# The last two attention units of a double-buffered einsum, loaded whole instead of in two halves

## The chip, the cores and the metric

The kernel runs on one core of a Trainium2 chip. The metric is the device time of one execution in microseconds; a kernel's time is the median of its runs. The profile is one further execution, recorded by the hardware profiler; its times count from the start of its own span.

## The reference

```python
batch, n_heads, seq, head_dim = 8, 12, 1024, 64
attn_weights: (8, 12, 1024, 1024) float32
v:            (8, 12, 1024, 64)   float32
out = np.einsum('bhqs,bhsd->bhqd', attn_weights, v).astype(np.float32)
```

For each of 96 heads, a 1024 x 1024 matrix of weights is multiplied by a 1024 x 64 matrix of values. The weights are 403 MB of float32, v and the output 25 MB each. There are few operations for each byte of the weights.

## The kernel before, in words

**Tiles.** Four heads make a group q, of which there are NV = 24. A group's weights are loaded as 128 partitions (4 heads x 32 row blocks), each with 32 rows of 1024. Half of that, G = 16 row positions, is one *unit* n; there are NU = 48 units, and unit n belongs to group n // 2. A unit is 8 MB of float32 in HBM; its load converts to bf16 on the way and writes 4 MB into `abf[n % 2]` (line 100), of which there are two. An even unit has i = 0, an odd one i = 1.

**What happens to a unit** (`pe_unit`, line 199). TensorE waits for the load (`s_abf`, line 201). It transposes the 16 positions, in 64 matmuls that go by line 144; pairs of bf16 are moved as one float32 word. Ahead of position GH = 8 it waits for `s_half` (line 204). VectorE and ScalarE copy the transposed tiles from PSUM to `at` (line 277). In an even unit, TensorE then spreads the four heads' v over partitions (line 161), and the copies of line 250 put it into `vbf`. Then it transposes the products of the unit before back (line 174), which ScalarE copies into `osb` (line 258) and counts in `s_out`, one for each unit. Last come the products of this unit (line 189), copied to `ot` by line 289. After unit 47 one more back transpose follows, whose two copies count in `s_fin`.

**Loads.** All loads of weights are issued from GpSimd's queue (POOL) by `load_attn` (line 341). The load of unit n + 2 is issued when the transposes of unit n have ended (line 396), because they free its buffer. So while a unit is worked on, the next one's load is under way. Units from `HALVED` on are loaded in two transfers of 8 row positions: the first counts in `s_abf`, the second in a semaphore of its own, `s_second[n]` (line 347).

**The gate s_half.** TensorE's wait ahead of the second half of unit n needs `s_half` of at least n + 1, counting units from 0. SyncE (SP) raises it: by `WHOLE[0]` at the start (line 410), by the next amount after each burst of stores (line 420), and by one for each halved unit when its second half has landed (lines 424 to 426). With `HALVED = NU - 2`, `ENDS` is 18, 34, 46 and `WHOLE` is 18, 16, 12; the last two units come from the loop in lines 424 to 426.

**Stores.** Products are gathered in `osb`, which has room for ten groups. The stores of groups 0 to 13 go in bursts from POOL's queue after units 16 and 32 (`BURSTS`, line 63). Four pairs of groups are left besides the last one, 2 MB each:

- q = 14 and q = 16, from POOL's queue, behind the last load (lines 401 and 402);
- q = 18 and q = 20, from SP's queue (lines 428 and 429). `store` (line 355) first waits for `s_out`: at least 41 for q = 18 and 45 for q = 20, which ScalarE reaches with the back copies of units 40 and 44;
- q = 22, the last pair, also from SP's queue, when `s_fin` is 2 (lines 430 and 431).

**The order on SP's queue** at the end is written out by hand:

```python
for n in range(HALVED, NU):
    nc.sync.wait_ge(s_second[n], 16)
    nc.sync.sem_inc(s_half)
nc.sync.wait_ge(s_osb, 16 * sum(len(x) for x in BURSTS.values()))
for q in range(BY_SYNC, NV - 2, 2):
    store(q, 2, nc.sync, s_end)
nc.sync.wait_ge(s_fin, 2)
store(NV - 2, 2, nc.sync, s_end, NU)
```

What stands ahead of this on SP are the waits for the transfers of v (line 422) and for the bursts (line 418).

Of the kernel before, what the change touches and what calls it, by code (L numbers as in the profile page):

```python
# [10 lines left out]
def kernel(  # L11
# [38 lines left out]
    NU = 2 * NV  # L50
# [8 lines left out]
    V_AT_ONCE = 4  # L59
    V_LOADS = {2: 2, **{q: V_AT_ONCE for q in range(V_AT_ONCE, NV, V_AT_ONCE)}}  # L60

    HALVED = NU - 2
    BURSTS = {8: ((0, 8),), 16: ((8, 2), (10, 4))}
    ENDS = [2 * q + 2 for q in BURSTS] + [HALVED]
    WHOLE = [n - m for m, n in zip([0] + ENDS, ENDS)]
# [50 lines left out]
    s_abf = [sem(f"s_abf{i}") for i in range(2)]  # L116
    s_second = {n: sem(f"s_second{n}") for n in range(HALVED, NU)}
    s_v0, s_v, s_cast = sem("s_v0"), sem("s_v"), sem("s_cast")
# [17 lines left out]
    with tc.tile_critical(sync_engine=mybir.EngineType.Pool, no_gpsimd_drain=True):  # L136
# [204 lines left out]
        def load_attn(n):  # L341
            pieces = [(0, G)] if n < HALVED else [(0, GH), (GH, GH)]
            for g0, gn in pieces:
                pool.dma_start(  # L344
                    out=abf[n % 2][:, ds(g0, gn)].rearrange("p g s -> p (g s)"),
                    in_=attn_q[n // 2][:, ds((n % 2 * G + g0) * S, gn * S)],
                ).then_inc(s_abf[n % 2] if g0 == 0 else s_second[n], 16)
# [66 lines left out]
        for k in range(1, NV // 2):  # L414
# [6 lines left out]
            if 2 * k in V_LOADS:  # L421
                nc.sync.wait_ge(s_v, 16 * (1 + list(V_LOADS).index(2 * k)))
                nc.sync.sem_inc(s_vr, V_LOADS[2 * k])
        for n in range(HALVED, NU):
            nc.sync.wait_ge(s_second[n], 16)
# [40 lines left out]
```

## Time and profile before

| | |
|---|---|
| Median of 3 runs | 1050.35 us (1050.28 to 1050.84) |
| Span of the profiled execution | 1048.8 us, on core 0 |
| TensorE matmul (PE), busy | 792.7 us, 76% |
| TensorE weight load (PEld), busy | 706.1 us, 67% |
| ScalarE (ACT), busy | 469.5 us, 45% |
| VectorE (DVE), busy | 389.3 us, 37% |
| GpSimd (POOL), busy | 36.9 us, 4% |
| HBM read and written | 427.82 MB and 25.17 MB, 432 GB/s over the span |
| Mean granted TensorE clock | 0.879 |
| Weights, whole loads | 46 issues of 4096 KB, 29.2 us median from issue to landing |
| Weights, half loads | 4 issues of 2048 KB, 22.8 us |
| Stores from POOL | 3 of 2048 KB (32.9 us), 1 of 4096 KB (41.6 us), 1 of 8192 KB (39.5 us) |
| Stores from SP | 3 of 2048 KB, 13.8 us median |

How to read it: the sizes and rates of the profile's DMA rows count the bytes written, so a load of 8 MB float32 counts as 4 MB. The profile has two DMA queues of interest, q0 for what GpSimd issues and q1 for what SyncE issues; both run on the same 16 engines. "DMA share" is the mean busy share of these engines; since the start and end of a packet fall into different stretches, it can be a little above 1 in a short one. In the chain of waits a line gives start, length and what it was; a DMA's piece ends where the transfer has landed. The time from issue to landing holds the time in which a transfer stands behind others. "PEclk" or "clock" is the share of its full clock that TensorE was granted.

### The profile page before, as it was taken

The page shows a single profiled execution, that of the slowest core. Times are in us where ns is not written, and L with a number is a line of the kernel's source. Part 1 is how long each engine was busy: PE and PEld are TensorE (multiplying, and loading weights), DVE is VectorE, ACT ScalarE, POOL GpSimd, SP SyncE. Part 2 cuts the span into 40 slices and gives each one's busy share as a digit, 9 for nine tenths or more (in the row PEclk, how much of TensorE's full clock was granted, in tenths as well). Part 3 has the DMA queues.
Part 4 walks back from the last instruction along what each step waited for, and adds up shares of the span by engine and source line. Part 5 has one row for each costly group of instructions (what it writes and reads, how often), then busy time and mean ns, then how long its engine had stood idle before and what let it go on. Part 6 is the DMA issues. An engine that isn't in the chain of part 4 may idle for free.

```text
span 1048.8 us, 17363 instructions
## 1 busy us (share of the span) xinstructions
PE 792.7 (76%) x7304; PEld 706.1 (67%) x7304; DVE 389.3 (37%) x584; ACT 469.5 (45%) x590; POOL 36.9 (4%) x68
## 2 busy tenths in 40 slices
PE   0978788479889393888949789748578884987994
PEld 0777687368778383777838588647567774867884
DVE  1443344234435151343515344324324332533542
ACT  0445355244545251354526355434335443544553
POOL 1000000000000000000000000000000000000000
PEclk9989799798999697889979899988778987998998
DMA  9999999999999999999999999999999999999999
GB/s 216 226 220 217 217 209 217 220 220 216 220 215 207 221 220 379 217 219 210 212 223 220 216 220 217 206 221 220 319 237 219 214 209 223 220 217 219 210 214 400
DMA packets 10662, 239.68 MB, mean 229 GB/s; under 512 B 1056, under 2 KB 1056, under 8 KB 1184
## 3 DMA queue, kind: packets, MB, share of 16 engines
q0 software_dynamic: 10080, 232.26, 98.9%
q1 hardware_dynamic: 576, 7.34, 1.7%
q8 instruction: 3, 0.05, 0.0%
q14 instruction: 3, 0.02, 0.0%
HBM read 427.82 MB, written 25.17 MB: 432 GB/s over the span
## 4 chain that ended last, share of the span: by engine, by line
DMA 71%; PE 26%; issue 1%; POOL 1%; ACT 0%; DVE 0%; SPq 0%; ACTq 0%; POOLq 0%
DMA abf<-in_attn_weights_dram 63%; PE bank L144 22%; DMA out_dram<-osb 8%; PE bank L161 3%; PE bank L189 1%; PE bank L174 0%; POOL vr L350 0%; DVE osb L258 0%; ACT vbf L250 0%; ACT osb L258 0%; POOL abf L344 0%; ACT ot L289 0%; POOL out_dram L358 0%; ACTq L258 0%; SPq L420 0%
## 5 line engine op out<-in xcount | busy, mean ns | idle before, releaser
L144 PE MATMUL bank<-ident,abf 128*128 128x128 f32 x3072 | 428.8, 307 | 213.0 <-DMA abf<-in_attn_weights_dram 189.5
L144 PEld LDWEIGHTS bank<-ident,abf 128*128 128x128 f32 x3072 | 419.1, 212 | 224.7 <-DMA abf<-in_attn_weights_dram 197.7
L277 DVE COPY at<-bank 128x1024 bf16<-128x1024 bf16 x480 | 319.6, 689 | 401.8 <-PE bank L144 395.2
L277 ACT COPY at<-bank 128x1024 bf16<-128x1024 bf16 x288 | 287.9, 1012 | 328.6 <-PE bank L144 328.6
L189 PE MATMUL bank<-at,vbf 128*64 128x256 bf16 x3072 | 225.5, 285 | 0.0
L189 PEld LDWEIGHTS bank<-at,vbf 128*64 128x64 bf16 x3072 | 203.6, 111 | 19.1 <-issue 6.1
L258 ACT COPY osb<-bank 64x512 f32 (+1 forms) x194 | 112.4, 580 | 28.1 <-PE bank L174 25.5
L289 DVE COPY ot<-bank 128x512 f32<-128x512 f32 x48 | 33.2, 692 | 207.1 <-PE bank L189 207.1
L161 PE MATMUL bank<-vr,spread 32*128 32x512 bf16 x768 | 87.0, 375 | 0.5 <-issue 0.2
L289 ACT COPY ot<-bank 128x512 f32<-128x512 f32 x48 | 28.1, 585 | 129.2 <-PE bank L189 129.2
L174 PE MATMUL bank<-ident,ot 128*128 128x128 f32 x392 | 61.3, 307 | 29.3 <-ACT vbf L250 28.7
L174 PEld LDWEIGHTS bank<-ident,ot 128*128 128x128 f32 x392 | 50.3, 157 | 41.4 <-ACT vbf L250 40.5
L161 PEld LDWEIGHTS bank<-vr,spread 32*128 32x128 bf16 x768 | 35.2, 93 | 43.9 <-issue 1.6
L250 ACT CAST vbf<-bank 128x512 bf16<-128x512 f32 x48 | 25.8, 588 | 74.3 <-PE bank L161 74.3
L344 POOL DMA_DIRECT2D abf<-in_attn_weights_dram x50 | 26.9, 537 | 816.1 <-PE bank L144 815.3
L250 DVE CAST vbf<-bank 128x512 bf16<-128x512 f32 x48 | 30.9, 686 | 29.1 <-PE bank L161 29.1
L277 ACT ACT_TABLE_LOAD x12 | 15.4, 1283 | 6.4 <-DMA osb<-in_v_dram 6.3
L350 POOL DMA_DIRECT2D vr<-in_v_dram x6 | 4.0, 675 | 132.9 <-PE bank L161 132.9
L358 POOL DMA_DIRECT2D out_dram<-osb x5 | 3.1, 620 | 7.5 <-ACT osb L258 7.5
L258 DVE COPY osb<-bank 64x512 f32<-64x512 f32 x2 | 1.4, 688 | 3.0 <-PE bank L174 3.0
L325 DVE MEMSET ident<- 128x128 f32 x1 | 0.2, 165 | 6.2 <-DMA osb<-in_v_dram 6.2
L332 DVE CAST vr<-osb 128x1024 bf16<-128x1024 f32 x2 | 2.2, 1138 | 0.0
(9 smaller groups left out, 5.1 us busy)
## 6 DMA issues: line engine op xcount, KB each, us to landing
abf<-in_attn_weights_dram POOLq DMA_DIRECT2D x46, 4096.0 KB, 29.2
vr<-in_v_dram POOLq DMA_DIRECT2D x5, 2048.0 KB, 15.8
out_dram<-osb POOLq DMA_DIRECT2D x1, 8192.0 KB, 39.5
abf<-in_attn_weights_dram POOLq DMA_DIRECT2D x4, 2048.0 KB, 22.8
out_dram<-osb POOLq DMA_DIRECT2D x3, 2048.0 KB, 32.9
out_dram<-osb SPq DMA_DIRECT2D x3, 2048.0 KB, 13.8
out_dram<-osb POOLq DMA_DIRECT2D x1, 4096.0 KB, 41.6
osb<-in_v_dram SPq DMA_DIRECT2D x1, 1024.0 KB, 5.1
```

The costliest lines, as they stand in the source:

```text
L144: last = pe.matmul(out=pt[g % 4][:, k], lhsT=words[:, k], rhs=ident, is_transpose=True, start=(k == 0), stop=(k == KW - 1),)
L161: last = pe.matmul(out=banks[h], lhsT=spread[rows, j, ds(VB - 1 - b, P)], rhs=vr[rows, n // 2, b], start=(b == 0), stop=(b == VB - 1),)
L174: last = pe.matmul(out=px[j0 // 4][:, ds(j * P, P)], lhsT=ot[:, j0 + j], rhs=ident, is_transpose=True, start=(j == 0), stop=(j == 3),)
L189: last = pe.matmul(out=outs, lhsT=vbf[:, 2 * kw + par, h], rhs=at[:, ds(half * GH, GH), kw, ds(h * VP, VP), par], start=(n == 0), stop=(n ...
L250: copy(out=vbf[:, :, h], in_=ps.rearrange("p (k d) -> p k d", k=SB)).then_inc(s_vbf)
L258: last = copy(out=rows[ds(n // 2 % 2 * HP, HP), ds(pp * 2 * G + n % 2 * G, G)].rearrange("p (half j) d -> p j half d", half=2)[:, ds(4 * k ...
L277: ins = copy(out=at[:, g].rearrange("c k j two -> c (k j two)"), in_=bank[g % 4].bitcast(bf16),)
L289: copy(out=ot.rearrange("c j (pp h p) -> c h j pp p", pp=2, h=VH)[:, ds(2 * e, 2)], in_=po[e].rearrange("c (h j p pp) -> c h j pp p", h=2, ...
L332: last = nc.vector.tensor_copy(out=vr_first[:, 0, part], in_=v32[:, part])
L344: pool.dma_start(out=abf[n % 2][:, ds(g0, gn)].rearrange("p g s -> p (g s)"), in_=attn_q[n // 2][:, ds((n % 2 * G + g0) * S, gn * S)],).th ...
L350: pool.dma_start(out=vr[:, ds(q % V_AT_ONCE // 2, fours // 2)].rearrange("p n b x -> p n (b x)"), in_=v_n(q, fours),).then_inc(s_v, 16)
L358: eng.dma_start(out=out_n(q, fours), in_=at_slot, **({"single_packet": True} if eng is pool and fours == 2 else {}),).then_inc(done, 16)
```

## The change

`HALVED` becomes `NU`, so that no unit is loaded in halves.

```diff
     V_LOADS = {2: 2, **{q: V_AT_ONCE for q in range(V_AT_ONCE, NV, V_AT_ONCE)}}
 
-    HALVED = NU - 2
+    HALVED = NU
     BURSTS = {8: ((0, 8),), 16: ((8, 2), (10, 4))}
     ENDS = [2 * q + 2 for q in BURSTS] + [HALVED]
```

The name is used in five places, and all follow from the one line. `ENDS` becomes 18, 34, 48, so `WHOLE` is 18, 16, 14: SP raises `s_half` to its final value 48 when the second burst has ended. `s_second` (line 117) has no members. `load_attn` makes one piece of every unit, with `s_abf` as its semaphore. The loop in lines 424 to 426 has no passes, so SP's queue goes from the waits for v straight to the wait on `s_osb` and the stores of q = 18 and 20. TensorE's instructions stay as they are.

## Prediction

> **What bounds the kernel now.** I read the page first, then the chain of waits at its end, then busy time by stage of the last 45 us. First the page:
>
> ```profile
> span 1048.8 us, 17363 instructions
> DMA  9999999999999999999999999999999999999999
> DMA 71%; PE 26%; issue 1%; POOL 1%; ACT 0%; DVE 0%; SPq 0%; ACTq 0%; POOLq 0%
> ```
>
> The DMA engines are busy in all 40 slices, and PE is on the chain for about a quarter of the span only. Anything that adds bytes to the stream ahead of the last load, or leaves the DMA engines empty, therefore shows. In the chain of waits the loads land like clockwork:
>
> ```profile
> 898.99 28.56 DMA abf<-in_attn_weights_dram
> ...
> 937.14 29.10 DMA abf<-in_attn_weights_dram
> ...
> 996.97 27.30 DMA abf<-in_attn_weights_dram
> ...
> 1036.24 0.69 DVE osb L258
> ```
>
> Start plus length is the landing: 927.55 and 966.24, so 38.69 for two units, 19.35 each. The last load lands at 1024.27, call it T. Then the second half's transposes run, and the last copy ends at 1036.93. Now the stages of the end (columns: stretch, its length, busy time of PE, PEld, DVE, ACT and POOL, clock, DMA share, GB/s):
>
> ```profile
> 983.00:1003.00 20.00, 20.00 (x213) 18.85 (x212) 8.71 (x13) 11.28 (x16) 2.12 (x4) 0.94 0.97 207
> 1022.00:1024.30 2.30, 1.62 (x14) 1.43 (x12) 1.93 (x3) 1.76 (x2) 0.00 (x0) 1.00 0.85 328
> 1024.30:1028.00 3.70, 3.65 (x30) 3.66 (x31) 2.38 (x5) 1.97 (x2) 0.00 (x0) 1.00 0.99 425
> 1044.00:1046.00 2.00, 0.00 (x0) 0.00 (x0) 0.00 (x0) 0.00 (x0) 0.00 (x0) 0.50 1.03 442
> 1046.00:1048.00 2.00, 0.00 (x0) 0.00 (x0) 0.00 (x0) 0.00 (x0) 0.00 (x0) 0.50 0.50 213
> ```
>
> After T the DMA engines are still full until about 1047, now at some 430 GB/s. (Loads show half of that, because the written bf16 bytes are counted.) What fills them is the stores: two from POOL, queued behind the last load, and three from SP. Five stores of 2 MB are 10.5 MB, and at 430 GB/s that is 24.4 us, which is the whole stretch from about 1022.5 (the rate begins to rise in 1022 to 1024.3) to 1047. So the end of the kernel is a full queue of stores, and PE's last work lies beside it. That is what the change touches.
>
> **The change, part by part.** With HALVED = NU no load has two pieces, no s_second exists, and SP's loop over n in (46, 47), lines 424 to 426, is empty. Three things follow.
>
> *The stores of q = 18 and q = 20 move.* This is the largest term. Both stand on SP's queue behind that loop. SP's waits (total, times, longest) and its two events say how long it held them:
>
> ```profile
> SPq L426 <- DMA abf<-in_attn_weights_dram: 154.6, 2, 135.3
> L426 SPq EVENT_SEMAPHORE x2: 17/17/17, 1005.0 to 1024.3; - x2
> 1024.41 12.88 SPq L358 DMA_DIRECT2D out_dram<-osb  x3
> 1036.96 0.33 SPq L358 DMA_DIRECT2D out_dram<-osb  x1
> ```
>
> SP came to the loop at 1005.0 - 135.3 = 869.7, saw load 46 landed at 1005.0 and load 47 19.3 later, and issued at 1024.41. Without the loop it stands at 869.7 in front of two waits only. The one on s_osb was met when the last burst ended, long before. The other is s_out of 41 for q = 18 and of 45 for q = 20: ScalarE's back copies in units 40 and 44:
>
> ```profile
> 904.87 2.35 ACT L258 COPY osb<-bank 64x512 f32 x4 [1.36 <-PE bank L174]
> 982.13 2.35 ACT L258 COPY osb<-bank 64x512 f32 x4 [0.90 <-PE bank L174]
> ```
>
> So the store of q = 18 goes out at 907.2, and that of q = 20 at 984.5 plus whatever the first one has delayed. Both then run in the middle of the load stream, where the DMA engines have nothing to spare (share 0.97 in 983 to 1003, the emptiest of the late stages). Their price, from the queues' share in 1024 to the end, 24.8 us, and in 1028 to 1035:
>
> ```profile
> q1 hardware_dynamic: 432, 6.29, 58.9%
> q1 hardware_dynamic: 99, 1.62, 54.2%
> q0 software_dynamic: 94, 1.44, 48.3%
> ```
>
> Three SP stores took 58.9% of 24.8 us, 14.6 us, so one is 4.9 us of all 16 engines. No row shows an SP store beside a load. From below a store would cost nothing (it fits into time that I cannot see), and below nothing is excluded, since the loads' bytes stay. From above I take twice the price, 9.8, for engines that turn from reading HBM to writing it at every packet. I take 4.9 each, since it is the row of the same transfer and the queues add up to 102% there: with work in both they share the engines about equally (99 packets against 94) and lose nothing. T becomes 1024.3 + 9.8 = 1034.1.
>
> Those two rows also say when the loads suffer. The Trainium skill, "DMA: Bandwidth & Descriptors", section "Queues, rings and completion order", has each engine take turns between queue rows, a whole packet each; the near-equal packet counts agree. By it the sum stays, and only the delay is spread.
>
> *Unit 46 starts later.* It now waits for its whole load. That landed at 1005.0, or 1009.9 with the first store ahead of it and 1014.8 with all of the second. The second goes out at about 984.5 + 4.9 = 989.4, some 20 us before, and takes turns with the load, so I take 1014.0. PE, from the timeline:
>
> ```profile
> 888.98 9.71 PE L144 MATMUL bank<-ident,abf 128*128 128x128 f32 x64 [13.46 <-DMA abf<-in_attn_weights_dram]
> ...
> 910.47 7.95 PE L144 MATMUL bank<-ident,abf 128*128 128x128 f32 x64
> ...
> 966.28 10.24 PE L144 MATMUL bank<-ident,abf 128*128 128x128 f32 x64 [6.02 <-DMA abf<-in_attn_weights_dram]
> ...
> 988.20 7.95 PE L144 MATMUL bank<-ident,abf 128*128 128x128 f32 x64
> ...
> 1001.37 7.95 PE L144 MATMUL bank<-ident,abf 128*128 128x128 f32 x64
> ...
> 1019.51 4.11 PE L144 MATMUL bank<-ident,abf 128*128 128x128 f32 x32
> 1024.35 4.11 PE L144 MATMUL bank<-ident,abf 128*128 128x128 f32 x32 [0.73 <-SPq L426]
> ...
> 1029.26 4.48 PE L189 MATMUL bank<-at,vbf 128*64 128x256 bf16 x64
> ```
>
> An even unit that follows a wait of several us takes 21.5 (unit 40, 888.98 to 910.47) or 21.9 (unit 44, 966.28 to 988.20); unit 46 without one took 18.1. In the changed kernel unit 45 would end at 1001.4 + 4.9 = 1006.3 and PE would idle 7.7, so I take 21.5: unit 47 begins at 1035.5, after T's 1034.1. The bounds are 1034.1 (18.1, then T decides) and 1036.7 (1014.8 and 21.9).
>
> *Unit 47 is done in one piece.* Before, 4.1 us of its transposes lay ahead of T, beside the landing of the second half; now all 64 follow the landing. An odd unit without a wait runs 988.20 to 1001.37, 13.2, against 1033.74 - 1024.35 = 9.4 from the second half's start. So it ends at 1035.5 + 13.2 = 1048.7. By itself this edit would cost almost nothing in the kernel before: the last store would go out some 4 us later, at about 1041, and four stores from 1022.5 on keep the engines full until 1042. With two of them gone that cover goes too.
>
> *The end.* From unit 47's last product to the last store's issue: 1036.96 - 1033.74 = 3.2, so it goes out at 1051.9. By then POOL's two stores, begun about T and worth 9.8, are done since some 1044, and the engines stand idle. What one store costs alone:
>
> ```profile
> osb<-in_v_dram SPq DMA_DIRECT2D x1, 1024.0 KB, 5.1
> DMA to landing us min/median/max: 11.8/13.8/19.0
> ```
>
> SP's 1 MB load at the start landed in 5.1, of which half of 4.9 is transfer, so 2.7 is around it; 4.9 + 2.7 = 7.6. The upper bound is 11.8, the last store of before, which still had others ahead of it. End: 1051.9 + 7.6 = 1059.5, against 1048.8. The median of the runs lies 1.55 above the profiled span, so 1061.0.
>
> *The pieces themselves.* POOL issues two transfers fewer; each was issued without delay and nobody waits for POOL there. Load 47 in halves landed 19.3 after load 46, and whole loads land 19.35 apart: no cost of halving to win back. The same skill page, section "Anatomy of one DMA — SWDGE (gpsimd) path", fits a fixed 2.0 us per DMA on GpSimd's path beside the bytes; two fewer would give back 4 us, and by it the sum would be 1057. The two spacings speak against it: queued transfers hide that part.
>
> **The rivals.**
>
> *The stores ride for free, or wait behind the loads.* SP's packets get only what the loads leave, so T stays at 1024.3 and the two stores end in the tail as before. Then unit 47 runs 1024.3 to 1037.5, the last store goes out at 1040.7, and the full queue ends at 1047 as now: 1050. If the stores are really free and early, 1040.7 + 7.6 = 1048.3 against 1048.8: 1050 again. With d the delay of T, the end is 1048.3 + d once the queue is empty, so it is no longer "no change" from d = 2.6 on, a quarter of the 9.8. Against it: 54.2% for SP beside 48.3% for POOL, and the full engines. For it: no row shows SP's stores against loads. That the stores do not move at all, because something else holds SP, comes to the same; I find no such wait.
>
> *Mixing costs more.* At twice the price T is 1043.9; unit 47 then starts at 1043.9 to 1046 and the end is 24 later: 1068 to 1070 on the span, about 1070 to 1072. In the bursts the kernel keeps loads away from stores (s_half), so no row prices it.
>
> *A gain.* The bytes stay and the engines are never empty before, so there is little to take. If the two stores were free and the last one cost its bare 4.9, the end would be 1040.7 + 4.9 = 1045.6, 1047 in the runs. And if every transfer held the engines for a while beside its bytes, two fewer would shorten the stream; the spacings of 19.3 and 19.35 leave 0.1 us for that at most. This is the skill page's fixed cost again, and here the measurement decides.
>
> **How the numbers follow.** Forecast, stores displacing loads at about their own price: 0.80. Free or held back: 0.08. Dearer than half again: 0.10. A gain: 0.02, nearly all of it for the stores. A measurement of this kernel can tell about 0.2%, 2.1 us, so faster 0.02, same 0.08, slower 0.90. The forecast's own range is 1058 (T decides, last store quick) to 1066 (11.8 for the last store); some of the cheaper and dearer prices for a store widen it to 1056 to 1067.
>
> **What would show it.** In the changed kernel SP should issue its first two stores near 907 and 989; load 42 should land about 5 us after the 927.55 of before and load 46 about 9 us after 1005.0; the last load should land near 1034; the last slice should no longer be full, with a hole of several us ahead of the last store, which goes out near 1052 and lands within 8 us. I am wrong if the last load lands before 1028 or after 1040, or if the DMA engines are full to the end.

## The result and the profile after

The changed kernel takes 1060.23 us (median of 5 runs, 1058.64 to 1062.62) against 1050.37 us before (median of 5): a ratio of 1.0093, 95% interval 1.0082 to 1.0104. It is slower by 9.9 us. The profiled execution has a span of 1059.1 us.

The chain of waits at the end of the changed kernel (start, length, what):

```profile
899.32 32.88 DMA abf<-in_attn_weights_dram
...
981.39 33.03 DMA abf<-in_attn_weights_dram
1014.42 0.04 issue
1014.47 10.24 PE bank L144 x64
...
1036.44 7.88 PE bank L144 x64
...
1051.41 0.68 DVE osb L258
```

Load 42 lands at 932.20 (927.55 before) and load 46 at 1014.42 (1005.0 before): 4.65 and 9.4 later. Each of the two lands 33 us after it was issued, in place of 28 to 29. Unit 47 begins at 1036.4, and its transposes follow unit 46 without a wait for data: at the end PE's own work is the chain. SP's queue says why the loads are late. Its three stores in one line (from the first issue to the end of the last), the second by itself, and how long a store took from issue to landing:

```profile
907.68 145.48 SPq L358 DMA_DIRECT2D out_dram<-osb  x3
...
989.53 0.33 SPq L358 DMA_DIRECT2D out_dram<-osb  x1
...
DMA to landing us min/median/max: 6.2/27.5/27.9
```

The first store goes out at 907.7 and the second at 989.5, both in the load stream, where they need 27.5 and 27.9 us to land. The wait on line 426 is gone. The third goes out at 1052.8 and lands in 6.2, with the engines to itself. What the first one takes from the loads is in the queues' rows for 907 to 940 (packets, MB, share of the time of all 16 engines):

```profile
q0 software_dynamic: 215, 6.19, 87.1%
q1 hardware_dynamic: 144, 2.10, 15.2%
```

The store (q1) took 15.2% of these 33 us, which is 5.0 us of all engines. The last load, too, is late. It was issued at 1001.0 and landed 33.3 us later, at 1034.3:

```profile
L344 POOL DMA_DIRECT2D abf<-in_attn_weights_dram x1: 528/528/528, 1001.0 to 1001.0; - x1
DMA to landing us min/median/max: 33.3/33.3/33.3
```

Busy time by stage (the last two columns are DMA share and GB/s):

```profile
1040.00:1042.00 2.00, 2.00 (x19) 2.00 (x18) 1.70 (x4) 1.53 (x2) 0.00 (x0) 1.00 1.07 459
1042.00:1044.00 2.00, 2.00 (x19) 2.00 (x18) 1.73 (x3) 1.57 (x3) 0.00 (x0) 1.00 0.24 98
1044.00:1046.00 2.00, 2.00 (x23) 1.81 (x23) 0.90 (x2) 1.96 (x3) 0.00 (x0) 1.00 0.00 0
1050.00:1052.00 2.00, 1.09 (x8) 0.86 (x8) 0.58 (x1) 1.24 (x3) 0.00 (x0) 1.00 0.00 0
1054.00:1056.00 2.00, 0.00 (x0) 0.00 (x0) 0.00 (x0) 0.00 (x0) 0.00 (x0) 0.50 0.93 393
```

From about 1043 to 1053 the DMA engines, which in the kernel before were full until about 1047, have nothing to do. That hole of some 10 us is the loss: two stores of 4.9 us each were taken out of the time beside PE's last unit, where they were free, and put into the load stream, where each pushes the last load, and with it PE's last work, back.

### The profile page after: what moved, and what is told of

Same layout as the page of the kernel before. It is cut to its first block, busy times and chain, and to the rows that moved or that the text cites. A ratio compares the mean times of both kernels' runs of the same rounds, so it can differ in the third digit from the quotient of the medians.

```text
span 1059.1 us, 17359 instructions
## 1 busy us (share of the span) xinstructions
PE 801.1 (76%) x7304; PEld 713.9 (67%) x7304; DVE 389.3 (37%) x584; ACT 469.6 (44%) x590; POOL 35.8 (3%) x66
## 4 chain that ended last, share of the span: by engine, by line
DMA 71%; PE 26%; issue 1%; POOL 0%; ACT 0%; DVEq 0%; DVE 0%; ACTq 0%; SPq 0%; POOLq 0%
DMA abf<-in_attn_weights_dram 63%; PE bank L144 22%; DMA out_dram<-osb 8%; PE bank L161 3%; PE bank L189 1%; PE bank L174 0%; POOL vr L350 0%; ACT osb L258 0%; ACT vbf L250 0%; DVEq L136 0%; DVE osb L258 0%; ACT ot L289 0%; POOL abf L344 0%; POOL out_dram L358 0%; ACTq L258 0%
## 5 line engine op out<-in xcount | busy, mean ns | idle before, releaser
L144 PE MATMUL bank<-ident,abf 128*128 128x128 f32 x3072 | 434.3, 310 | 220.4 <-DMA abf<-in_attn_weights_dram 198.3
L144 PEld LDWEIGHTS bank<-ident,abf 128*128 128x128 f32 x3072 | 424.8, 212 | 231.9 <-DMA abf<-in_attn_weights_dram 206.1
## 6 DMA issues: line engine op xcount, KB each, us to landing
out_dram<-osb SPq DMA_DIRECT2D x3, 2048.0 KB, 27.5
```

Of the source, the lines that this page charges most:

```text
L144: last = pe.matmul(out=pt[g % 4][:, k], lhsT=words[:, k], rhs=ident, is_transpose=True, start=(k == 0), stop=(k == KW - 1),)
```

## The experiments

Theory A: the moved stores are the cause. Theory B: loading a unit whole is. Theory C: taking reads and writes in turn costs beyond the bytes. The diffs of the experiments are against the changed kernel.

**Whole loads, stores late** (one part of the change alone).

```diff
+        nc.sync.wait_ge(s_abf[1], 16 * NV)
         for q in range(BY_SYNC, NV - 2, 2):
             store(q, 2, nc.sync, s_end)
```

> Both units whole, but SP waits for the last load to land (s_abf[1] of 16 NV) before it issues the stores of q = 18 and 20, as it did with the halves. Theory A (what costs time is that these two stores move into the load stream): the last load lands near 1024.3 as before; unit 46 starts at the landing of its whole load, 1005, and takes about 19.4; unit 47 starts at about 1024.4, the last store goes out at about 1040.8, and the full queue of five stores ends near 1047: 1050.4, no change from before. Theory B (whole loads cost time because PE can begin only when all has landed): up to the 4 us of half a unit's transposes at the end, 1054, or all of the loss, 1060.

Measured: 1050.70 (11 runs), ratio to before 1.0004, interval 0.9995 to 1.0013. TensorE, and the DMA share around the last store's issue:

```profile
1004.99 10.00 PE L144 MATMUL bank<-ident,abf 128*128 128x128 f32 x64 [4.72 <-DMA abf<-in_attn_weights_dram]
...
1026.72 7.95 PE L144 MATMUL bank<-ident,abf 128*128 128x128 f32 x64
```

```profile
1040.00:1042.00 2.00, 1.09 (x8) 0.86 (x8) 0.24 (x1) 1.24 (x3) 0.00 (x0) 1.00 0.99 426
1042.00:1044.00 2.00, 0.00 (x0) 0.00 (x0) 1.14 (x2) 0.49 (x1) 0.00 (x0) 0.99 0.27 115
1044.00:1046.00 2.00, 0.00 (x0) 0.00 (x0) 0.00 (x0) 0.00 (x0) 0.00 (x0) 0.50 1.21 516
```

Theory B falls. With two more stores in the end's queue, whole loads are hidden, though only just: unit 46 took 21.7 and not 19.4, and the queue had just run dry (0.27 in 1042 to 1044) when the last store came, at 1043.2.

**Halves, stores early** (the other part alone): HALVED = NU - 2 again, and SP's loop behind the stores.

```diff
-    HALVED = NU
+    HALVED = NU - 2
...
-        for n in range(HALVED, NU):
-            nc.sync.wait_ge(s_second[n], 16)
-            nc.sync.sem_inc(s_half)
         nc.sync.wait_ge(s_osb, 16 * sum(len(x) for x in BURSTS.values()))
         for q in range(BY_SYNC, NV - 2, 2):
             store(q, 2, nc.sync, s_end)
+        for n in range(HALVED, NU):
+            nc.sync.wait_ge(s_second[n], 16)
+            nc.sync.sem_inc(s_half)
```

> The kernel before with its halves, but SP issues the stores of q = 18 and 20 ahead of its waits for the second halves. Theory A: the last load lands near 1034, 9.8 later, and the last slice is empty for some us. The halves then help, because PE and no longer the queue of stores sets the end: unit 46's second half at 1014 leads to its end near 1028.5, the second half of unit 47 starts at 1034.1, its products end 9.4 later, the last store goes out at 1046.7 and lands 6.2 later: 1052.9 on the span, 1054.5. If the position of the stores were the whole cost whatever the halves do: 1060. Theory B (halving alone matters): 1050.4, as before.

Measured: 1056.07, ratio 1.0054 (1.0041 to 1.0068). So moving the stores costs 5.7 us with halves and 9.5 with whole loads (1060.23 against 1050.70), while halves are worth 0.3 with late stores (no difference by the interval) and 4.2 with early ones. The two edits are not additive: nothing measurable of the 9.9 us is left when the stores are late again, and 4.2 of it goes when the halves come back. The expectation was 1.6 low:

```profile
1005.55 4.11 PE L144 MATMUL bank<-ident,abf 128*128 128x128 f32 x32
1015.46 5.37 PE L144 MATMUL bank<-ident,abf 128*128 128x128 f32 x32 [5.79 <-SPq L429]
...
1032.46 7.95 PE L144 MATMUL bank<-ident,abf 128*128 128x128 f32 x64
```

Unit 46's second half started at 1015.5, and from there to unit 47 it took 17.0, where 14.5 was reckoned. By the time TensorE came to unit 47's second half, at about 1036.5, that had landed (1034.8): PE set the end, not the landing.

**One store early.**

```diff
         for q in range(BY_SYNC, NV - 2, 2):
+            if q > BY_SYNC:
+                nc.sync.wait_ge(s_abf[1], 16 * NV)
             store(q, 2, nc.sync, s_end)
```

> The changed kernel, but only the store of q = 18 is early; that of q = 20 waits for the last load. Theory A: last load at 1029.2, one store price of 4.9 later than before; unit 46 starts at 1009.9 after a wait of some 3.6 and takes 19.4 to 21.5; unit 47 starts at 1029.3 to 1031.4; last store out at 1045.7 to 1047.8, lands 6.2 later: 1053.5 to 1055.5, about half of the loss. Theory C (each switch between reads and writes costs beyond the bytes): the last load lands later than 1030. Theory B: 1060, as the changed kernel.

**Four stores early.**

```diff
-        for q in range(HELD_FROM, BY_SYNC, 2):
-            store_2(q)
...
-        for q in range(BY_SYNC, NV - 2, 2):
-            store(q, 2, nc.sync, s_end)
+        for q in range(HELD_FROM, NV - 2, 2):
+            store(q, 2, nc.sync, s_held if q < BY_SYNC else s_end)
```

> The changed kernel with twice as many early stores: those of q = 14 and 16 also go from SP, as soon as SP is free and their groups are done, near 869.7, in place of POOL's place behind the last load. Theory A (each 2 MB store ahead of the last load delays it by its own 4.9 us, and the end hangs on PE's last units): last load at 1043.9, last store out near 1062 and landing 6.2 later: 1068 on the span, 1070; the steps 0, 1, 2 and 4 early stores give 1050.4, 1055.3, 1060.2 and 1070. Theory C (reads and writes in turn cost more than the bytes): above 1073. If the loss of the changed kernel had another cause than these stores: 1060.

Measured: 1055.26 with one (ratio 1.0041, 1.0025 to 1.0056) and 1069.60 with four (1.0181, 1.0166 to 1.0197). Four kernels with whole loads and all stores, by the number of stores ahead of the last load:

| early stores | 0 | 1 | 2 | 4 |
|---|---|---|---|---|
| median, us | 1050.70 | 1055.26 | 1060.23 | 1069.60 |
| unit 46 begins, us | 1004.99 | 1009.94 | 1014.47 | 1024.68 |

Unit 46's start, with one and with four early:

```profile
1009.94 10.10 PE L144 MATMUL bank<-ident,abf 128*128 128x128 f32 x64 [6.16 <-DMA abf<-in_attn_weights_dram]
```

```profile
1024.68 9.44 PE L144 MATMUL bank<-ident,abf 128*128 128x128 f32 x64 [9.24 <-DMA abf<-in_attn_weights_dram]
```

Each further store costs 4.6 to 5.0 us in the time and delays the start of unit 46 by 4.5 to 5.1: about the 4.9 that it takes by itself. Theory C, at any price that would matter, falls too. (The two stores moved from POOL's queue also lose `single_packet`, which `store` sets for POOL's pairs only; their price is that of stores from SP.)

**Two stores left out.**

```diff
-        for q in range(BY_SYNC, NV - 2, 2):
-            store(q, 2, nc.sync, s_end)
...
-    nc.vector.wait_ge(s_end, 16 * (NV - BY_SYNC) // 2)
+    nc.vector.wait_ge(s_end, 16)
```

> The changed kernel without the stores of q = 18 and 20: those four groups each of the output are not written, so its time is that of a kernel with less to do. It shows what the two stores take from the load stream. Theory A: the last load lands at 1024.3, 9.8 earlier than in the changed kernel, unit 47 starts at about 1024.4, the last store goes out at 1040.8 into empty engines and lands 6.2 later: 1047.0 on the span, 1048.5. Theory B: the end is as late as in the changed kernel, 1059 to 1060, since whole loads stay.

Measured: 1050.22 (10 runs, 1048.47 to 1051.53), ratio to before 0.9995 (0.9986 to 1.0005). It is 10.0 faster than the changed kernel, as A says, and 1.7 above A's number:

```profile
1005.37 10.24 PE L144 MATMUL bank<-ident,abf 128*128 128x128 f32 x64 [5.97 <-DMA abf<-in_attn_weights_dram]
...
1027.28 7.95 PE L144 MATMUL bank<-ident,abf 128*128 128x128 f32 x64
```

Unit 46 took 21.9, so unit 47 began some 3 us after its load. And 4 MB less to write gained nothing measurable over the kernel that writes them late: there they really were free.

**Only unit 47 halved**, a candidate: `HALVED = NU - 1`.

> HALVED = NU - 1: unit 46 whole, unit 47 in halves, and SP again held until the last half has landed. Candidate for a version as good as the kernel before. Theory A: the last load lands at 1024.3; unit 46 begins at 1005 and runs at a low clock, unit 47 begins near 1026.7 as in the kernel with whole loads and late stores; the queue of stores hides it: 1050.4 to 1050.7, no difference. If the halves were what the time hangs on, it would lie near 1055.

Measured: 1050.58 (11 runs), ratio 1.0004 (0.9995 to 1.0013). It is as good as the kernel before, not better. No version in this study beats the kernel before.

**Only unit 46 halved, stores early.** Which half gives back the 4.2 us?

```diff
-    HALVED = NU
+    HALVED = NU - 2
...
-    s_second = {n: sem(f"s_second{n}") for n in range(HALVED, NU)}
+    s_second = {NU - 2: sem("s_second")}
...
-            pieces = [(0, G)] if n < HALVED else [(0, GH), (GH, GH)]
+            pieces = [(0, G)] if n != NU - 2 else [(0, GH), (GH, GH)]
...
-        for n in range(HALVED, NU):
-            nc.sync.wait_ge(s_second[n], 16)
-            nc.sync.sem_inc(s_half)
...
         for q in range(BY_SYNC, NV - 2, 2):
             store(q, 2, nc.sync, s_end)
+        nc.sync.wait_ge(s_second[NU - 2], 16)
+        nc.sync.sem_inc(s_half, 2)
```

> The stores of q = 18 and 20 early, unit 46 in halves, unit 47 whole. With both in halves 1056.1 was measured and with both whole 1060.2. Theory A1 (what the halves give back is that PE starts unit 46 ahead of its landing): unit 46 ends near 1032.5, unit 47 starts at the landing of its load, 1034.1 at most, the last store goes out 16.5 later, 1050.6, and lands 6.2 later: 1056.8 on the span, 1058.3 or less. Theory A2 (it is the second half of unit 47 that gains): 1060.

Measured: 1060.37, ratio 1.0095 (1.008 to 1.0111). That is A2's number, but the trace shows another reason:

```profile
1027.02 4.48 PE L189 MATMUL bank<-at,vbf 128*64 128x256 bf16 x64
1034.34 10.56 PE L144 MATMUL bank<-ident,abf 128*128 128x128 f32 x64 [2.84 <-DMA abf<-in_attn_weights_dram]
```

Unit 46 ended at 1031.5, earlier than expected, and unit 47 started with its landing at 1034.3. But after a wait of 2.84 its transposes took 10.6 in place of 7.9, and all was lost again. So halving unit 46 alone lets PE be early, but gives it nothing to do until load 47 lands. Halving unit 47 alone, with the stores early, was not run. In the changed kernel unit 47 begins at 1036.4, about 2 us after its whole load has landed, which speaks against any gain there. That both halves are needed is argued from these traces.

**TensorE kept busy while it waits.** Four runs ask about that slow unit, each with unused transposes of the identity ahead of the wait for the load, as

```diff
+            if i == 0:
+                for x in range(48):
+                    pe.matmul(
+                        out=pt[0][:, x % KW],
+                        lhsT=ident,
+                        rhs=ident,
+                        is_transpose=True,
+                        start=(x % KW == 0),
+                        stop=(x % KW == KW - 1),
+                    )
             pe.wait_ge(*loaded)
```

> The changed kernel, with 48 more transposes of the identity matrix (results unused, overwritten) ahead of the wait for the load in every even unit, some 6 us of work in a time in which TensorE otherwise waits. It asks why an even unit takes 21.5 to 21.9 after a wait and 18.1 without one. If the wait itself lowers the granted clock: unit 46 takes 18.1 to 19.4, unit 47 then starts at the landing of the last load, 1034.1, in place of 1036.4, and the time is 1058, 2 less than the changed kernel. If the low clock has another cause: 1060.2, unit 46 still above 21.

> The changed kernel, with unused transposes of the identity only in the last pass of TensorE's loop: 72 of them (8.1 us at 112 ns) ahead of unit 46's wait for its load, where TensorE waited 8.5, and 16 (1.8 us) ahead of unit 47's. If a wait of several us is what lowers the clock: unit 46 starts at 1014.5 and takes 18.1, unit 47 starts at 1034.1 to 1034.5 at the full clock, the last store goes out 16.5 later, 1050.8, and lands 6.2 later: 1057.0 on the span, 1058.5, about 2 less than the changed kernel. If the low clock has another cause: unit 46 takes over 21, unit 47 starts behind its transposes at 1038, and the time is 1062.

> Stores early, unit 46 in halves, unit 47 whole, and 28 unused transposes (3.1 us) ahead of unit 47's wait in the last pass, where TensorE waited 2.8 and then took 10.6 in place of 7.9 for the transposes of unit 47. If the wait lowers the clock: unit 47 starts at 1034.3 to 1034.6 and takes 13.2, last store out at 1050.8 to 1051.1, landing 6.2 later: 1057.0 to 1057.3 on the span, 1058.6, about 2 less than the same kernel without them (1060.4). If not: 1060.4.

> As the kernel with unused transposes in the last pass, but with the 72 ahead of unit 46 alone; the 16 ahead of unit 47 had outlasted the wait they were to fill. Unit 46 then ends at 1034.2, at about the landing of the last load. If the low clock in unit 46 is what the changed kernel loses beside the landing: unit 47 starts at 1034.2 to 1034.5, last store out at 1050.7 to 1051.0, landing 6.2 later: 1057.1 on the span, 1058.6, 1.6 less than the changed kernel. If the clock drops in unit 47 in its place, as it did behind a wait of 2.8 with unit 46 in halves: 1060 to 1061.

In the last three the added transposes stand under `pe.If(it > NV - 1)`, so in the last pass only. Measured: 1060.36 with 48 in every even unit; 1059.85 with 72 and 16 at the end; 1059.46 with unit 46 halved and 28; 1059.10 with 72 alone (ratio to before 1.0081, 1.0067 to 1.0095). The first three missed their aim. The 48 did not outlast the wait for unit 46; unit 44 of the same run, which followed its transposes without a wait, shows the difference:

```profile
967.00 5.46 PE L203 MATMUL bank<-ident 128*128 128x128 f32 x48
972.30 7.85 PE L144 MATMUL bank<-ident,abf 128*128 128x128 f32 x64
...
1015.66 10.54 PE L144 MATMUL bank<-ident,abf 128*128 128x128 f32 x64 [5.66 <-DMA abf<-in_attn_weights_dram]
```

The 16 and the 28 ran until 1036.0 and 1035.7, beyond the landing of load 47 (1034.3). The 72 alone fitted:

```profile
1005.91 8.08 PE L204 MATMUL bank<-ident 128*128 128x128 f32 x72
1014.52 7.95 PE L144 MATMUL bank<-ident,abf 128*128 128x128 f32 x64 [0.53 <-DMA abf<-in_attn_weights_dram]
...
1028.25 4.48 PE L189 MATMUL bank<-at,vbf 128*64 128x256 bf16 x64
1034.37 7.95 PE L144 MATMUL bank<-ident,abf 128*128 128x128 f32 x64 [1.64 <-DMA abf<-in_attn_weights_dram]
```

Unit 46 took 18.2, as it did without a wait before, then PE waited for load 47, which landed at 1034.33. The last store went out at 1050.8 in place of 1052.8, took 6.9 us to land in place of 6.2, and the span was 1057.8 against 1059.1. Part of this is not due to the edit: the kernel with 72 and 16 does the same up to the end of unit 46, and there the unit took 19.7. In the medians the 1.1 us against the changed kernel is within the intervals, so what the slow unit 46 costs the changed kernel is not settled by the times.

## Why the prediction was right, point by point

- **The stores move.** Forecast at 907.2 and 989.4; the first went out at 907.7, the second at 989.5. Confirmed, and the first experiment shows it as the cause: with the stores late, nothing measurable of the loss is left. That the loss is as large as 9.9 needs the whole loads too; with halves the same move costs 5.7.
- **The price of one, 4.9, taken from the tail's row.** Load 47's landing moves from 1024.3 to 1034.3, 10.0 for two against 9.8 forecast; the queue's own row gives 5.0 for the first; and the table of 0, 1, 2 and 4 stores is close to a straight line. Neither bound, nothing or twice, was near.
- **The equal shares** nearly held in packets, but not in time. From 908 to 935, with the first store under way, its 144 packets stand beside 166 of the loads, but 18.5% of the engines' time beside 82.8%: by these figures a packet of the store took 0.56 us and one of the loads 2.2. With 9 packets on each of the 16 engines, taken in turn, that makes an estimate of 9 x 2.7 = 24 us, near the 27.5 that it needed. The sum did not rest on this.
- **Unit 46** was put at 1014.0 and 21.5 and came at 1014.47 and 21.9. That PE's slow unit and not the landing starts unit 47 was right: 1036.4 measured, 1035.5 forecast, with the load there since 1034.3.
- **Unit 47 and the last store.** 13.2 forecast, 13.2 measured (1036.4 to 1049.6); out at 1052.84, not 1051.9.
- **The last store alone** was mis-sized: 6.2, not 7.6. SP's 1 MB load at the start, from which the 2.7 around a transfer was taken, ran beside the first loads of the weights. This error of 1.4 and the 0.9 of lateness nearly cancel, so the total (a span of 1059.5 forecast, 1059.1 measured; a time of 1061.0 and 1060.23) looks better than its terms: that much was luck.
- **Whole loads by themselves cost almost nothing.** Shown by the first experiment, but the margin was thinner than reckoned: the last store went out at 1043.2, not 1041. The sum for this case, and the one for the rival of free stores, let unit 47 start at the landing, 1024.3, and left out the slow unit 46 that the main sum had; unit 47 began at 1026.7. So the 1048.3 of that rival was about 2 us low: without the two stores the span was 1050.1.
- **What the prediction did not price**: that with the stores early the halves are worth 4.2. It said that their cover goes, and left it there. Only the 2 x 2 of the two edits showed it.
- The rival "free, or waits behind" fails on the landings, "dearer" on the straight line, and "a gain" on the time. (The DMA share of 0.97, called the emptiest of the late stages, was not quite that: 1010 to 1014 has 0.96 and 1022 to 1024.3 has 0.85. Nothing rests on it.) Halving has no cost to win back: with the stores late or left out, load 46 came at 1004.7 to 1005.3 whole, and at 1005.0 in halves.

## What to carry to other kernels

A wait in a queue also places everything behind it. Here one constant removed a wait that looked like part of the halving, and the two stores behind it went where the engine they share is full. When a resource is busy all the time, work is not free or dear by its size but by its place: ahead of the last item that others wait for it can cost its full time, behind that item it can be free. Ask of every edit near the end what else was hidden by the same queue, and test two coupled edits each alone.

## What was not expected of the hardware

TensorE's clock after a wait. Over the whole spans of all thirteen traces, the 64 transposes of line 144 stand 581 times together in one row. They took 7.85 to 7.96 us in the 270 cases without a wait ahead of them and in the 33 after a wait of 0.43 to 1.73 us. After each of the 278 waits of 1.87 us and more, up to 25.5, they took 9.07 to 10.56. The two nearest to the limit, in the kernel with halves and early stores and in the kernel before:

```profile
439.80 7.95 PE L144 MATMUL bank<-ident,abf 128*128 128x128 f32 x64 [1.73 <-DMA abf<-in_attn_weights_dram]
```

```profile
782.61 9.44 PE L144 MATMUL bank<-ident,abf 128*128 128x128 f32 x64 [1.87 <-DMA abf<-in_attn_weights_dram]
```

In the kernel with unit 46 halved, the granted clock behind the 2.84 us was 0.50 for some 6 us:

```profile
1034.00:1036.00 2.00, 1.66 (x8) 1.66 (x9) 0.49 (x1) 0.00 (x0) 0.00 (x0) 0.50 0.99 426
1036.00:1038.00 2.00, 2.00 (x11) 2.00 (x10) 0.89 (x2) 1.01 (x1) 0.00 (x0) 0.50 1.02 434
1038.00:1040.00 2.00, 2.00 (x12) 2.00 (x11) 0.92 (x2) 1.01 (x1) 0.00 (x0) 0.50 1.05 451
1040.00:1042.00 2.00, 2.00 (x17) 2.00 (x16) 1.38 (x3) 1.01 (x1) 0.00 (x0) 0.88 0.98 418
```

The Trainium skill, "TensorE: Matmul & The Clock Gate", section "HAM oscillation — how this bites in real kernels", warns of idle gaps above some 3.4 us; here waits from 1.87 us on were enough every time, and none up to 1.73 was. Unused transposes held the clock up where they closed the gap: with the 72 alone it was 1.00 in every stage from 1003 to 1044. What stays open is the rest of the unit: with 72 and 16 unused transposes unit 46 began at full speed, and yet its back transposes took 1.81 in place of 1.09 some 13 us later, behind a wait of 1.20, while with the 72 alone they did not. This may be why the changed kernel's runs spread over 4.0 us where those of the kernel before stay within 0.6 (five runs each): with a full queue the end did not hang on TensorE's clock, now it does. That was argued, not tested.
